# A hybrid decoder layer on one core: small vectors requested by GpSimd, x scaled on ScalarE, and K tiles grouped 3, 4, 4, 5

## The chip, the cores and the metric

One core of a Trainium2 chip runs the whole program. The engines are TensorE (PE in the profile; its weight loads are PEld), VectorE (DVE), ScalarE (ACT), GpSimd (POOL) and SyncE (SP), which here issues the loads from memory. The metric is the time of one launch in microseconds (us), the median of several executions. Differences under about 0.2% (2.6 us) are not distinguishable from none.

## What is computed

One layer on 256 tokens of width 2048. The part that matters here is its head:

```
mod = silu(c) @ w_mod + b_mod                  # w_mod 2048 x 12288; six rows of 2048
sh1, sc1, g1, sh2, sc2, g2 = split(mod)
h = rmsnorm(x, norm_mix) * (1 + sc1) + sh1
proj = h @ w_in                                # w_in 2048 x 5660
# proj feeds four token mixers: gated linear attention, gated DeltaNet, pooling, forgetting attention
y = concat(mixers) @ w_out;  x = x + g1 * y
h = rmsnorm(x, norm_ffn) * (1 + sc2) + sh2
x = x + g2 * (silu(conv(h @ w_gate)) * (h @ w_up)) @ w_down
out = rmsnorm(x, norm_final)
```

All arithmetic is float32 in effect: each weight tile is split into a rounded high part and the low remainder, and a product is made of three matmuls (high-high, high-low, low-high).

## The kernel before

The 2048 inputs of the first projection are 16 tiles of 128, the K tiles. They are visited in four groups (`GROUPS`, four tiles each). For a group the first stage needs the shift and scale (sh1, sc1) of its tiles, which is a product of one row, silu(c), with all 2048 rows of w_mod: `mods4` loads 16 tiles `wm` (128 partitions, two runs of 512 columns, 512 KB each), and VectorE adds each into `ga` with the factor from silu(c) (line 103). When the 16th is in, 8 products of `ga` with a column of ones (16 matmul instructions, "ext<-ones,ga") turn the sums into columns `md`, three VectorE rows finish `md`, ScalarE makes h of each tile from the transposed x, and `split` writes its high and low part into `bigA`. Only then can matmuls of this group's tiles run.

What a group's tiles feed is of two kinds. `gdn(g)` multiplies them with 1536 columns of w_in into six accumulators `acc` that stay in PSUM over all groups. `extras(g)` visits the last `TAKE[g]` of 16 column pairs (256 columns each) and adds the group's part to their sums in SBUF (rows "pr<-ext,pr" on VectorE). What is not visited early is made up after the last group, between the steps of the mixers. Each piece of w_in is loaded as `wr` (five buffers), and `split` gives `wh` (ScalarE cast, line 115) and `wl` (VectorE subtraction, line 100), three buffers each, before the matmul (line 97). While a group's matmuls run, the generator `nxt` brings in the next group's `wm` tiles, one per step.

Small vectors (convolution weights, norms, biases, constants `ct`, the rows `hrow`, and the 28 narrow columns of w_in as `wsm`) are requested by `rest` and `small_load` during the first group, on SP's queue among the large loads; `rest` also transposes some of them on TensorE. `small` and `gates` use them at the last group. GpSimd has 23 rows of its own in the whole program.

The order on each engine is set by a list scheduler from the order of the code and its own estimate of times, and each engine then runs its list in that order: an instruction that waits holds up everything behind it on its engine.

Of the kernel before, what the change touches and what calls it, by code (L numbers as in the profile page):

```python
# [42 lines left out]
K_N = K_LV + 128  # L43


GROUPS = ((0, 4), (4, 4), (8, 4), (12, 4))
NG = len(GROUPS)

TAKE = (16, 12, 11)

ORDER = "gpfd"

ON_PE, PE_RATE = "s0 s1 h0", 0.38
ON_DVE, DVE_RATE = "h1 g0 g1", 0.69


def _consts():
# [16 lines left out]
def trunk_kernel(ctx: ExitStack, tc: tile.TileContext, x, c, w_mod, b_mod, norm_mix, norm_ffn, w_in,  # L74
# [153 lines left out]
    with ExitStack() as ph:  # L228
# [59 lines left out]
        with ExitStack() as st:  # L288
# [29 lines left out]
                act(flat(pr[:, 0:8]), xt[:, t], AF.Square, accum_out=ssm[:, t:t + 1])  # L318
            tsc(ssm[:, 2:4], ssm[:, 0:2], 1.0 / D, EPS, ALU.mult, ALU.add)
            G.tensor_tensor(out=ssm[:, 0:2], in0=ssm[:, 2:4], in1=mhalf[:, 0:2], op=ALU.pow)  # L320
# [12 lines left out]


            def mods(g):
                for k0 in range(GROUPS[g][0], sum(GROUPS[g]), 4):
                    yield from mods4(k0, min(4, sum(GROUPS[g]) - k0))

            def mods4(k0, nk):
                n = nk * P  # L340

                def f(ga):
                    b = ext()
                    for i in range(2 * nk):
                        mm(b[:, i:i + 1], ga[:, i * P:i * P + P], ones[:, 0:1])
                    md = sp.tile([P, 2 * nk], F32, name="md", tag="md", bufs=2, padded_shape=[P, 16])
                    tt(md[:, 0:nk], b[:, 0:nk], bm(0, k0, nk), ALU.add)
                    tt(md[:, nk:], b[:, nk:2 * nk], bm(1, k0, nk), ALU.add)
                    tt(md[:, nk:], md[:, nk:], nmix[:, k0:k0 + nk], ALU.mult)
                    for kk in range(nk):  # L350
                        k = k0 + kk
                        h = sp.tile([P, T], F32, name="h", tag="h", bufs=2)
                        act(h, xnT[:, k], AF.Identity, scale=md[:, nk + kk:nk + kk + 1], bias=md[:, kk:kk + 1])
                        split(HL[:, k, 0:T], HL[:, k, T:], h)
                views = [wm_v[:, k, 0:2 * D].rearrange("p (s n) -> p s n", n=D)[:, :, P * k0:P * k0 + n]
                         for k in range(KT)]
                ga = keep.tile([P, 2 * n], F32, name="ga", tag="ga", padded_shape=[P, 1024])
                for k in range(KT):
                    wm = sp.tile([P, 2 * n], F32, name="wm", tag="wm", bufs=5, padded_shape=[P, 1024])
                    last_wm[0] = nc.sync.dma_start(wm.rearrange("p (s n) -> p s n", n=n), views[k])  # L360
                    accumulate(ga, wm, k)
                    if k == KT - 1:
                        with tc.high_priority():
                            f(ga)
                    yield

            def rest():
                nc.sync.dma_start(wlr[0:16], gla_w_lr[0])
                nc.sync.dma_start(wlr[28:29], gla_b_lr)
                nc.sync.dma_start(r2[0:48], gdn_conv[0].rearrange("j (k p) -> (j k) p", p=P))  # L370
                nc.sync.dma_start(r2[48:52], pool_scale[0].rearrange("(k p) -> k p", p=P))
                nc.sync.dma_start(r2[52:53], gla_norm)
                nc.sync.dma_start(r2[53:54], gdn_norm)
                nc.sync.dma_start(ct, cst[:, P:K_N])
                row = lambda ap: ap.partition_broadcast(P).rearrange("p o h -> p (o h)")
                nc.sync.dma_start(hrow[:, 0:4], row(gdn_a_log))
                nc.sync.dma_start(hrow[:, 4:8], row(gdn_dt_bias))
                nc.sync.dma_start(hrow[:, 8:12], row(fox_f_bias))
                nc.sync.dma_start(r3, ffn_conv_w[0, 0:2].rearrange("j (k p) -> (j k) p", p=P))
                nc.sync.dma_start(r4[0:NF], ffn_conv_w[0, 2].rearrange("(k p) -> k p", p=P))  # L380
                nc.sync.dma_start(r4[NF:], ffn_conv_b[0].rearrange("(k p) -> k p", p=P))
                b = ext()
                PE.transpose(b[:, 0:54], r2, ident[0:54, 0:54])
                S_.copy(V2, b[:, 0:54])
                b = ext()
                PE.transpose(b[:, 0:2 * NF], r3, ident[:2 * NF, :2 * NF])
                PE.transpose(b[:, 2 * NF:4 * NF], r4, ident[:2 * NF, :2 * NF])
                S_.copy(V3, b[:, 0:3 * NF])
                S_.copy(CB, b[:, 3 * NF:4 * NF])
                S_.copy(idr, ident)  # L390
                S_.copy(ngr, K(K_NEG))
                for i, m_ in enumerate(up + lw):
                    G.tensor_scalar(out=m_, in0=K(K_LV), scalar1=float(i + 1), scalar2=None, op0=ALU.is_equal)


            def small_load():
                nc.sync.dma_start(wsm[:, :, 0:16], wi_v[:, :, C_LR:C_LR + 16])
                nc.sync.dma_start(wsm[:, :, 16:24], wi_v[:, :, C_B:C_B + 8])
                nc.sync.dma_start(wsm[:, :, 24:28], wi_v[:, :, C_FF:C_FF + 4])
                split(wsh, wsl, wsm)  # L400

            def small():
                o = ext()[0:28, 0:T]
                for k in range(KT):
                    mm(o, wsh[:, k], HL[:, k, 0:T], start=k == 0, stop=False)
                    mm(o, wsh[:, k], HL[:, k, T:], start=False, stop=False)
                    mm(o, wsl[:, k], HL[:, k, 0:T], start=False, stop=k == KT - 1)
                S_.copy(smT[0:28], o)

            def gdn(g):  # L410
                k0, nk = GROUPS[g]
                for k2 in range(k0, k0 + nk, 2):
                    for c3 in range(3):
                        wh, wl = load_split(wi_v, k2, 2, C_QKV + 512 * c3, 512)
                        for kk in range(2):
# [22 lines left out]
            def pair(p, g0, g1):  # L438
                c0, tok, dst, scale = pairs[p]
                k0, k1 = GROUPS[g0][0], sum(GROUPS[g1 - 1])  # L440
                a = ext().rearrange("p (f t) -> p f t", t=T)
                for ka in range(k0, k1, 4):
                    kb = min(ka + 4, k1)
                    wh, wl = load_split(wi_v, ka, kb - ka, c0, 256)
# [12 lines left out]
                    yield  # L457
# [46 lines left out]

            bgt = lambda: bgp.tile([P, 512], F32, name="bgt", tag="bgt")
            bg = [marked(jobs(ON_PE, bgt)), jobs(ON_DVE, None)]
            for _ in mods(0):
                pass
            hold = [last_wm[0]]
            for g in range(NG):  # L510
                nxt = mods(g + 1) if g < NG - 1 else iter(())
                with tc.issue_after(hold[0].ins):
# [1 line left out]
                        small()  # L514
                        gates()
                    for i, _ in enumerate(gdn(g)):
                        next(nxt, None)
                        if g == 0 and i == 2:
                            rest()
                            small_load()  # L520
                    if g == NG - 1:
                        break
                    for _ in extras(g):
                        next(nxt, None)
# [605 lines left out]
```

## Time and profile before

| | us |
|---|---|
| median of 3 runs (1309.63 to 1311.2) | 1309.63 |
| profiled execution, its own time | 1305.91 |
| span of the profiled execution | 1304.1 |
| TensorE busy | 1251.1 (96%) |
| VectorE busy | 893.8 (69%) |
| ScalarE busy | 638.1 (49%) |
| GpSimd busy | 23.5 (2%) |

The page gives busy time by engine, the span in 40 slices, the chain of work that ended last, and groups of equal instructions with mean duration and the idle time ahead of them. Besides it the trace answers by window (busy time, granted TensorE clock, and memory traffic in a stretch) and by timeline (instructions in order of time, with what ended the idle time ahead of each). 1.8 us of the profiled execution lie outside its span.

### The profile page before, as it was taken

The numbers are of one execution on the slowest core, as the hardware profiler recorded it, in microseconds if no ns is written. First come the engines' busy times: TensorE is split into PE (matmuls) and PEld (weight loads), VectorE is DVE, ScalarE is ACT, GpSimd is POOL, SyncE is SP. The second block draws the span as 40 slices with busy tenths as digits, with TensorE's granted clock in tenths as the row PEclk, the third lists the DMA queues.
The fourth block names the chain that finished last, engine by engine and source line by source line (L and its number), as shares of the span: only waits on it lengthen the run. The fifth ranks groups of instructions, "written<-read, shape, count | busy, mean of one in ns | idle before, by whom it ended". The sixth has DMA issues, their size and how long they took to land.

```text
span 1304.1 us, 20373 instructions
## 1 busy us (share of the span) xinstructions
PE 1251.1 (96%) x7927; PEld 1094.0 (84%) x7927; DVE 893.8 (69%) x1201; ACT 638.1 (49%) x1000; POOL 23.5 (2%) x31
## 2 busy tenths in 40 slices
PE   2799999999999999999999999999999999999996
PEld 1799999898876788888888888888888888888896
DVE  7679797989763397676656565765666597974543
ACT  3455344774354444565545554555555454443432
POOL 0200000010000100000000000000000000000000
PEclk8799999999999999999999999999999999999998
DMA  8999998796567997466666666666666699875652
GB/s 324 287 367 376 321 335 295 257 335 216 163 236 242 325 331 262 146 183 189 186 187 191 182 176 197 191 184 188 190 184 181 193 372 366 316 249 193 193 180 81
DMA packets 174231, 311.94 MB, mean 239 GB/s; under 512 B 16172, under 2 KB 65331, under 8 KB 173495
## 3 DMA queue, kind: packets, MB, share of 16 engines
q1 hardware_dynamic: 174135, 310.65, 73.3%
q8 instruction: 62, 1.02, 0.3%
q14 instruction: 34, 0.28, 0.1%
HBM read 308.51 MB, written 2.10 MB: 238 GB/s over the span
## 4 chain that ended last, share of the span: by engine, by line
PE 92%; DMA 5%; DVE 1%; ACT 1%; issue 1%; SPq 1%; POOLq 0%; ACTq 0%; DVEq 0%
PE fpt L97 57%; PE ext L97 16%; PE wot L97 5%; PE acc L97 4%; PE gdt L97 4%; DMA wm<-in_w_mod_dram 4%; PE bgt L97 3%; PE oxt L97 2%; DVE ga L103 1%; DMA wr<-in_w_in_dram 1%; DMA wsm<-in_w_in_dram 0%; ACT xT L1011 0%; DVE wl L100 0%; ACT wh L115 0%; PE oxt L873 0%
## 5 line engine op out<-in xcount | busy, mean ns | idle before, releaser
L100 DVE TENSOR_TENSOR wl<-wr,wh 128x1024 fp32r<-128x1024 f32 x384 | 468.4, 1223 | 294.2 <-ACT wh L115 293.2
L115 ACT CAST wh<-wr 128x1024 fp32r<-128x1024 f32 x384 | 402.5, 1051 | 491.4 <-PE fpt L97 306.6
L97 PE MATMUL fpt<-bigA,wh 128*128 128x512 f32 x1408 | 485.7, 397 | 2.1 <-DVE bigA L103 2.1
L97 PE MATMUL fpt<-bigA,wl 128*128 128x256 f32 x1408 | 376.2, 281 | 0.0
L97 PEld LDWEIGHTS fpt<-bigA,wh 128*128 128x128 f32 x1408 | 261.1, 188 | 62.5 <-issue 2.2
L97 PEld LDWEIGHTS fpt<-bigA,wl 128*128 128x128 f32 x1408 | 259.7, 188 | 4.8
L103 DVE SCALAR_TENSOR_TENSOR ga<-wm,cond,ga 128x1024 f32<-128x1024 f32 x139 | 177.8, 1279 | 11.3 <-DMA wm<-in_w_mod_dram 10.3
L97 PE MATMUL fpt<-wl,AH 128*128 128x512 f32 (+1 forms) x440 | 152.9, 348 | 0.0
L97 PE MATMUL fpt<-wh,AL 128*128 128x512 f32 (+1 forms) x440 | 152.5, 347 | 0.0
L97 PE MATMUL fpt<-wh,AH 128*128 128x512 f32 (+1 forms) x440 | 142.6, 348 | 0.0
L97 PE MATMUL ext<-bigA,wh 128*128 128x256 f32 x768 | 137.1, 280 | 0.0
L97 PEld LDWEIGHTS ext<-bigA,wh 128*128 128x128 f32 x768 | 117.3, 189 | 3.1 <-DVE dS L100 0.8
L97 PE MATMUL ext<-bigA,wl 128*128 128x256 f32 x384 | 107.4, 280 | 1.7 <-DVE wl L100 1.7
L97 PEld LDWEIGHTS fpt<-wh,AH 128*128 128x128 f32 x440 | 83.3, 189 | 10.8 <-ACT wh L115 0.2
L97 PEld LDWEIGHTS fpt<-wh,AL 128*128 128x128 f32 x440 | 83.3, 189 | 10.6 <-issue 0.2
L97 PEld LDWEIGHTS fpt<-wl,AH 128*128 128x128 f32 x440 | 83.3, 189 | 10.5 <-issue 0.2
L97 PEld LDWEIGHTS ext<-bigA,wl 128*128 128x128 f32 x384 | 72.1, 188 | 3.0 <-DVE wl L100 1.9
L97 PE MATMUL acc<-bigA,wh 128*128 128x256 f32 x384 | 69.0, 286 | 3.5 <-ACT bigA L115 2.8
L97 PE MATMUL ext<-wh,bigA 128*128 128x256 f32 (+1 forms) x320 | 69.5, 309 | 0.0
L97 PE MATMUL wot<-wh,bigA 128*128 128x512 f32 (+1 forms) x256 | 63.0, 337 | 0.0
L97 PEld LDWEIGHTS acc<-bigA,wh 128*128 128x128 f32 x384 | 59.6, 195 | 3.9 <-ACT bigA L115 2.9
L97 PEld LDWEIGHTS ext<-wh,bigA 128*128 128x128 f32 x320 | 53.0, 193 | 5.5 <-ACT wh L115 1.7
(340 smaller groups left out, 1187.4 us busy)
## 6 DMA issues: line engine op xcount, KB each, us to landing
wm<-in_w_mod_dram SPq DMA_DIRECT2D x192, 512.0 KB, 6.3
wr<-in_w_in_dram SPq DMA_DIRECT2D x88, 512.0 KB, 9.1
wr<-in_ffn_w_gate_dram SPq DMA_DIRECT2D x88, 512.0 KB, 4.0
wr<-in_ffn_w_up_dram SPq DMA_DIRECT2D x88, 512.0 KB, 3.9
wr<-in_ffn_w_down_dram SPq DMA_DIRECT2D x88, 512.0 KB, 4.4
wr<-in_w_out_dram SPq DMA_DIRECT2D x32, 512.0 KB, 4.4
xt<-in_x_dram SPq DMA_DIRECT2D x2, 1024.0 KB, 7.1
bigC<-in_x_dram SPq DMA_DIRECT2D x2, 1024.0 KB, 10.5
```

The lines of the kernel that those rows point to most:

```text
L97: PE.matmul(o, lhsT=l, rhs=r, start=start, stop=stop, skip_group_check=True)
L100: V.tensor_tensor(out=o, in0=a, in1=b, op=op)
L103: V.scalar_tensor_tensor(out=o, in0=a, scalar=s, in1=b, op0=op0, op1=op1)
L115: S_.copy(hi, src)
```

## The change

- The groups are 3, 4, 4 and 5 K tiles. A group of five is cut by `runs` into runs of at most four for the shift and scale and for the column pairs (3 and 2) and of at most two for the DeltaNet columns (2, 2 and 1). `ahead` advances the next group's generator once per run of that group.
- 16, 13 and 12 column pairs are visited early in place of 16, 12 and 11.
- The two VectorE multiplications that scale x by its norm become four ScalarE activations on half rows.
- All 16 small requests leave SP's queue for GpSimd's. They stand behind a GpSimd instruction that is new, the last multiplication of the second group's `md`. The split of `wsm` moves into `small`, and the transposes and masks of `rest` behind the third group.

```
-GROUPS = ((0, 4), (4, 4), (8, 4), (12, 4))
+GROUPS = ((0, 3), (3, 4), (7, 4), (11, 5))
-TAKE = (16, 12, 11)
+TAKE = (16, 13, 12)
+def runs(k0, n, most):
+    m = -(-n // most)
+    cut = [k0 + (n * i + m - 1) // m for i in range(m + 1)]
+    return [(a, b - a) for a, b in zip(cut, cut[1:])]
...
-            for t in range(NT):
-                tsc(xt[:, t], xt[:, t], ssm[:, t:t + 1], None, ALU.mult)
+            for hs in (slice(0, D // 2), slice(D // 2, D)):
+                for t in range(NT):
+                    act(xt[:, t, hs], xt[:, t, hs], AF.Copy, scale=ssm[:, t:t + 1])
...
-                    tt(md[:, nk:], md[:, nk:], nmix[:, k0:k0 + nk], ALU.mult)
+                    if k0 == GROUPS[1][0]:
+                        asked[0] = G.tensor_tensor(out=md[:, nk:], in0=md[:, nk:], in1=nmix[:, k0:k0 + nk], op=ALU.mult)
+                    else:
+                        tt(md[:, nk:], md[:, nk:], nmix[:, k0:k0 + nk], ALU.mult)
...
+            def rest_load():
+                G.dma_start(wlr[0:16], gla_w_lr[0])
...
+            def ahead(g, nxt):
+                for _ in range(len(runs(*GROUPS[g + 1], 4)) if g < NG - 1 else 0):
+                    next(nxt, None)
...
                     for i, _ in enumerate(gdn(g)):
-                        next(nxt, None)
-                        if g == 0 and i == 2:
-                            rest()
-                            small_load()
+                        ahead(g, nxt)
...
+                if g == 0:
+                    with tc.issue_after(asked[0].ins):
+                        small_load()
+                        rest_load()
+                if g == 2:
+                    rest()
```

On SP, in the first group, the last small requests stood ahead of the fourth piece of w_in (`wr`); before:

```order
L379 DMA r3_112<-in_ffn_conv_w_dram 88x128
L380 DMA r4_113<-in_ffn_conv_w_dram 44x128
L381 DMA r4_113<-in_ffn_conv_b_dram 44x128
L397 DMA wsm_115<-in_w_in_dram 128x16x16
L398 DMA wsm_115<-in_w_in_dram 128x16x8
L399 DMA wsm_115<-in_w_in_dram 128x16x4
L155 DMA wr_417<-in_w_in_dram 128x2x512
L360 DMA wm_447<-in_w_mod_dram 128x2x512
```

and now, from the third piece on:

```order
L162 DMA wr_340<-in_w_in_dram 128x2x512
L374 DMA wm_337<-in_w_mod_dram 128x2x512
L162 DMA wr_373<-in_w_in_dram 128x512
L374 DMA wm_370<-in_w_mod_dram 128x2x512
L162 DMA wr_394<-in_w_in_dram 128x512
L374 DMA wm_391<-in_w_mod_dram 128x2x512
```

The 16 small requests are gone from this queue, and the odd third tile of the group is loaded in single-tile pieces.

On ScalarE, the rows that use the small vectors moved from the first group into the second. `wsh` is the cast of `wsm`, `ngr` that of a piece of `ct`, `ea` the exponential of `hrow`; now they stand so among the casts of the weight pieces:

```order
L122 CAST wh_929<-wr_927 128x1024
L444 COPY pr_92<-ext_859 128x512
L122 CAST wsh_116<-wsm_115 128x448
L444 COPY pr_92<-ext_885 128x512
L122 CAST wh_963<-wr_961 128x1024
L122 CAST wh_996<-wr_994 128x1024
L122 CAST wh_1029<-wr_1027 128x1024
L122 CAST wh_1062<-wr_1060 128x1024
L407 CAST ngr_91<-ct_85 128x128
L119 ACT_TABLE_LOAD
L119 ACTIVATE ea_2385<-hrow_89 128x4
L122 CAST wh_1095<-wr_1093 128x1024
```

Here `wh_929` and the next five are the six pieces of DeltaNet weights of the second group; `wsh` stands behind the first of them, `ngr` and `ea` behind the fifth.

On VectorE, the rows that finish the first group's `md` were and are:

```order
L100 TENSOR_TENSOR wl_280<-wr_277,wh_279 128x1024
L100 TENSOR_TENSOR wl_314<-wr_311,wh_313 128x1024
L100 TENSOR_TENSOR md_257<-ext_248,V1_73 128x4 x2
L107 TENSOR_SCALAR ga_307<-wm_308,cond_77 128x1024
L100 TENSOR_TENSOR md_257<-md_257,V1_73 128x4
```

```order
L107 TENSOR_TENSOR wl_276<-wr_273,wh_275 128x1024
L107 TENSOR_TENSOR md_257<-ext_250,V1_73 128x3 x2
L107 TENSOR_TENSOR wl_310<-wr_307,wh_309 128x1024
L107 TENSOR_TENSOR md_257<-md_257,V1_73 128x3
L114 TENSOR_SCALAR ga_303<-wm_304,cond_77 128x1024
```

The second subtraction now stands between the rows of `md`, and the first row of the next group's sum behind them.

More of the change, by code (lines that the diff above doesn't have):

```diff
@@ L335, in mods @@
             def mods(g):
-                for k0 in range(GROUPS[g][0], sum(GROUPS[g]), 4):
-                    yield from mods4(k0, min(4, sum(GROUPS[g]) - k0))
+                for k0, nk in runs(*GROUPS[g], 4):
+                    yield from mods4(k0, nk)
+            asked = [None]
             def mods4(k0, nk):
@@ L396, in small_load, with small @@
             def small_load():
-                nc.sync.dma_start(wsm[:, :, 0:16], wi_v[:, :, C_LR:C_LR + 16])
-                nc.sync.dma_start(wsm[:, :, 16:24], wi_v[:, :, C_B:C_B + 8])
-                nc.sync.dma_start(wsm[:, :, 24:28], wi_v[:, :, C_FF:C_FF + 4])
+                for o, c, n in ((0, C_LR, 16), (16, C_B, 8), (24, C_FF, 4)):
+                    G.dma_start(wsm[:, :, o:o + n], wi_v[:, :, c:c + n])
+            def small():
                 split(wsh, wsl, wsm)
-            def small():
                 o = ext()[0:28, 0:T]
@@ L410, in gdn @@
             def gdn(g):
-                k0, nk = GROUPS[g]
-                for k2 in range(k0, k0 + nk, 2):
+                for k2, nk in runs(*GROUPS[g], 2):
                     for c3 in range(3):
-                        wh, wl = load_split(wi_v, k2, 2, C_QKV + 512 * c3, 512)
-                        for kk in range(2):
+                        wh, wl = load_split(wi_v, k2, nk, C_QKV + 512 * c3, 512)
+                        for kk in range(nk):
                             k = k2 + kk
@@ L441, in pair @@
                 a = ext().rearrange("p (f t) -> p f t", t=T)
-                for ka in range(k0, k1, 4):
-                    kb = min(ka + 4, k1)
-                    wh, wl = load_split(wi_v, ka, kb - ka, c0, 256)
+                for ka, nk in sum((runs(*GROUPS[g], 4) for g in range(g0, g1)), []):
+                    kb = ka + nk
+                    wh, wl = load_split(wi_v, ka, nk, c0, 256)
                     for f in range(2):
@@ L523, in trunk_kernel @@
                     for _ in extras(g):
-                        next(nxt, None)
+                        ahead(g, nxt)
                 for _ in nxt:
```

27 lines of the change are left out of this document (13 added, 14 removed).

## The prediction

> **What bounds the kernel now.** I read the page first, then the windows, then the timeline of the first 220 us.
>
> ```profile
> PE 1251.1 (96%) x7927; PEld 1094.0 (84%) x7927; DVE 893.8 (69%) x1201; ACT 638.1 (49%) x1000; POOL 23.5 (2%) x31
> ```
>
> TensorE is busy for all but 53 us of 1304.1, and both instruction orders hold the same 7427 matmuls, so only its idle time, its slow clock and new waits can move the end. The windows (columns: busy time of PE, PEld, DVE, ACT, POOL, then granted clock, share and rate of memory traffic) say where the loss is.
>
> ```profile
> 10.00:20.00 10.00, 4.62 (x18) 3.35 (x19) 8.20 (x10) 3.22 (x6) 0.70 (x1) 1.00 0.98 348
> 20.00:30.00 10.00, 2.61 (x16) 1.91 (x15) 9.35 (x9) 2.77 (x5) 0.00 (x0) 0.72 0.96 338
> 30.00:42.00 12.00, 3.54 (x16) 3.49 (x16) 9.71 (x12) 4.46 (x7) 0.00 (x0) 0.50 1.04 372
> 42.00:48.10 6.10, 6.08 (x26) 5.75 (x27) 3.88 (x6) 3.75 (x9) 4.10 (x6) 0.50 0.61 93
> 50.00:60.00 10.00, 8.50 (x72) 8.13 (x71) 5.44 (x5) 3.76 (x6) 1.57 (x3) 1.00 0.97 335
> 60.00:75.00 15.00, 13.31 (x110) 12.91 (x109) 11.85 (x11) 6.84 (x9) 0.00 (x0) 1.00 1.08 366
> 42.00:98.20 56.20, 52.65 (x405) 51.42 (x406) 38.42 (x37) 26.39 (x38) 7.32 (x12) 0.91 0.99 321
> 98.20:162.70 64.50, 62.81 (x550) 62.62 (x550) 53.85 (x57) 29.55 (x37) 0.00 (x0) 1.00 1.02 348
> 162.70:215.20 52.50, 52.50 (x449) 52.50 (x449) 48.88 (x55) 22.27 (x26) 0.00 (x0) 1.00 0.98 330
> 215.20:262.00 46.80, 45.52 (x379) 40.86 (x378) 41.95 (x88) 29.57 (x55) 1.45 (x3) 1.00 0.79 254
> ```
>
> Until 42 us memory runs at 338 to 372 GB/s while TensorE is mostly idle: the head waits for loads. From 42 to 48 the clock is 0.50 and traffic falls to 93 GB/s. TensorE idles another 1.50 and 1.69 us up to 75. Afterwards it is full or nearly so, with VectorE at 48.88 of 52.50 and memory at 330 to 348 GB/s close behind. The timeline shows the steps of the head and the ends of the first three groups' sums (the `md` rows).
>
> ```profile
> 4.20 24.69 SPq L360 DMA_DIRECT2D wm<-in_w_mod_dram  x16
> 17.39 1.23 ACT L328 COPY bigC<-ext 128x512 f32<-128x512 f32 x2 [5.92 <-PE ext L327]
> 22.30 1.09 ACT L328 COPY bigC<-ext 128x512 f32<-128x512 f32 x2 [0.24 <-PE ext L327]
> 31.47 0.88 SPq L368 DMA_DIRECT2D wlr<-in_gla_w_lr_dram  x1
> 34.28 1.29 DVE L103 SCALAR_TENSOR_TENSOR ga<-wm,cond,ga 128x1024 f32<-128x1024 f32 x1 [0.47 <-DMA wm<-in_w_mod_dram]
> 35.71 3.54 PE L97 MATMUL ext<-ones,ga 128*128 128x1 f32 x16 [12.94 <-DVE ga L103]
> 39.29 0.23 DVE L100 TENSOR_TENSOR md<-ext,V 128x4 f32<-128x4 f32 x2
> 40.10 0.16 DVE L100 TENSOR_TENSOR md<-md,V 128x4 f32<-128x4 f32 x1
> 42.02 1.65 PE L97 MATMUL acc<-bigA,wh 128*128 128x256 f32 x6 [2.77 <-ACT bigA L115]
> 43.66 0.40 SPq L397 DMA_DIRECT2D wsm<-in_w_in_dram  x1
> 47.79 2.07 SPq L155 DMA_DIRECT2D wr<-in_w_in_dram  x1
> 50.87 0.57 ACT L115 CAST wsh<-wsm 128x448 fp32r<-128x448 f32 x1 [3.86 <-DMA wsm<-in_w_in_dram]
> 98.12 0.23 DVE L100 TENSOR_TENSOR md<-ext,V 128x4 f32<-128x4 f32 x2 [1.08 <-PE ext L97]
> 162.70 0.22 DVE L100 TENSOR_TENSOR md<-ext,V 128x4 f32<-128x4 f32 x2
> 215.15 0.22 DVE L100 TENSOR_TENSOR md<-ext,V 128x4 f32<-128x4 f32 x2
> ```
>
> The sixteenth wm tile ends VectorE's wait at 34.28; sums, columns and h follow, and the first matmul of a product starts at 42.02. The sums are made against this execution (span 1304.1, itself 1305.91 with 1.8 outside the span) and then taken off the median, 1309.63, which lies 3.7 above it.
>
> **Three tiles first.** Sixteen tiles of 384 in place of 512 KB are 2.10 MB less. At 355 GB/s, between the rows' 338 and 372, that is 5.9 us. The last sum row is shorter:
>
> ```profile
> L103 DVE SCALAR_TENSOR_TENSOR xt<-bigC,V,xt 128x253 f32<-128x253 f32 x12 | 5.6, 469 | 0.0
> L112 ACT ACTIVATE pr<-xt 128x2048 f32<-128x2048 f32 x2 | 3.8, 1910 | 2.8 <-DMA xt<-in_x_dram 2.8
> 168.70 1.28 DVE L103 SCALAR_TENSOR_TENSOR ga<-wm,cond,ga 128x1024 f32<-128x1024 f32 x1
> 169.90 0.68 DVE L100 TENSOR_TENSOR pr<-ext,pr 128x512 f32<-128x512 f32 x1
> 170.50 1.21 DVE L100 TENSOR_TENSOR wl<-wr,wh 128x1024 fp32r<-128x1024 f32 x1
> 171.63 0.42 DVE L100 TENSOR_TENSOR bigA<-h,bigA 128x256 fp32r<-128x256 f32 x1
> 171.96 1.28 DVE L103 SCALAR_TENSOR_TENSOR ga<-wm,cond,ga 128x1024 f32<-128x1024 f32 x1
> ```
>
> From 469 ns at 253 columns and 1280 at 1024 it costs 1.05 ns a column, so 768 columns save 0.27. Twelve column products in place of 16, at 3.54/16 = 0.22, save 0.9. Against it, the subtraction that now stands between the md rows pushes their last one back: 0.15 + 1.13 where 0.81 stands now, +0.5. The first product matmul comes 6.6 earlier, at 35.4.
>
> **ScalarE scales x.** Four half rows at 1.91/2 are 3.8 us. They lie in ScalarE's 5.92 of idle time before 17.39; the last copy of the transposed x, begun by 23, may end 2 us later, and its reader (h) starts only after md, past 33. VectorE's rows that leave the head were followed by waits for loads. Cost and gain nothing; without the 8 us of cover, up to 2.
>
> **The first group.** From 42.02 to 98.12 are 56.1 us for 384 matmuls. The pitch, from 162.70 to 215.15 with 432 matmuls, is (52.45 - 1.8)/432 = 0.117, where 1.8 is for 16 column products at full clock (half of 0.22 each). So 46.7 is work; 9.4 is excess: 3.05 for 6.1 us at half clock, 3.2 idle in the 50:60 and 60:75 rows, the rest small transposes and dips. The changed order has 288 matmuls here: 33.7 + 1.8. The clock will again have dropped (TensorE idles before the sums), so 3.0 stays. Of the other 6.4 I take half off: SP no longer spends 31.47 to 47.79 mostly on small requests, and the fourth wr no longer waits for them until 47.79. That gives 41.7, and the group's sums end at 77.1; between 38.5 and 44.9.
>
> On the clock the Trainium skill (TensorE: Matmul & The Clock Gate, The HAM clock gate) says some 3.4 us of sustained work release it; the row has 6.1. By the rule 1.3 us less would be lost; the row decides.
>
> **The second group.** 492 matmuls: 57.6 + 1.8, and 1.0 of excess as in 98.12 to 162.70 (528: 63.6 of 64.6). It ends at 137.5. VectorE, by the steps of the next part, has 15 sums, 19 long and 5 short subtractions and 10 adds: 18.0 + 21.5 + 4.3 + 6.0 and 2.8 of small rows, 52.6; it was 53.85 and stays under TensorE. The last md row on GpSimd is 0.5 us longer than on VectorE by its nearest row (below), while TensorE still has pairs of the old group to do: nothing.
>
> **Five tiles in two pieces.** This is where the early gain is partly given back. TensorE has 460 matmuls and 20 column products: 53.8 + 2.2 = 56.0. VectorE's steps, from start to start in the rows above, are 1.20 for a sum, 0.60 for an add, 1.13 for a subtraction, 0.33 for bigA; by 1.05 ns a column a sum of 768 steps 0.93, of 512 0.66. The order holds 15 + 15 of these sums, their two first rows (1.0), 19 subtractions, 13 adds, 7 bigA and 0.8 of md: 14.0 + 9.9 + 1.0 + 21.5 + 7.8 + 2.3 + 0.8 = 57.3. VectorE becomes the longer one. It can't be gapless (48.88 of 52.50 is the most it had), so I take 59.0, between 57.3 and 61.6 (57.3 at that share). The third sums' end: 196.5.
>
> At that point 1240 matmuls are done, against 1344 at 215.15; 104 at 0.117 are 12.2, so the same work stood at 203.0 before. Small transposes still to come take off 0.4. **Sum: 203.0 - 0.4 - 196.5 = 6.1 us earlier.** After it TensorE was busy for 45.52 of 46.80, and what is left of pairs fills the mixers as before, so the gain stays. The span would be 1298.0, the median 1303.5.
>
> **GpSimd's requests.** This price the trace doesn't show. ScalarE takes wsh, ngr and ea in order, so a late request stops every wh behind it. From the end of the second group's sums TensorE has 132 matmuls until it needs wh_963, 15.4 us; less about 2 for md and the first request and 1.6 for two casts, the three wsm may take 11.7 us. For ea, behind thirteen requests, the same count (228 matmuls) leaves 21.8. From below: SP's three took 7.2 (43.66 to 50.87). From above:
>
> ```profile
> L393 POOL TENSOR_SCALAR mk<-ct 128x128 uint8<-128x128 f32 x12 | 7.3, 615 | 31.8 <-DMA ct<-in_cst_dram 31.2
> L320 POOL TENSOR_TENSOR ssm<-ssm,mhalf 128x2 f32<-128x2 f32 x1 | 0.7, 696 | 11.5 <-DVE ssm L109 11.5
> ```
>
> GpSimd takes 615/128 = 4.8 ns a column; if it made each of the 2048 short runs of a wsm request at that pace, three would take 29.5. I take the lower end, since the transfers are the same ones: hidden.
>
> **Rivals.** (1) *GpSimd's requests are late.* For it: 6144 runs of 64, 32 and 16 bytes from an engine that has made no request so far, and ScalarE's order, which lets nothing pass wsh. Against it: SP's 7.2. It decides from 11.7 us for three wsm; beyond that TensorE idles one for one, and from 17.8 the whole gain is gone. At 29.5 it costs 17.8: 1321.3. Where it ends on the slow side, taken halfway from 17.8 to 29.5 at 23.7, 12.0 are lost: 1315.5. The first thing seen would be ACT's wsh or ea idle behind a DMA.
> Of this the Trainium skill (DMA: Bandwidth & Descriptors, Anatomy of one DMA) gives about 2.0 us of fixed cost for a request made by GpSimd. If they followed one another without overlap, thirteen would be an estimated 26 us, 4 over the 21.8, and the time 1307.7; no run here shows it yet.
>
> (2) *Memory becomes the bound.* The second group and the two pieces need 8.4 + 10.7 + 0.8 and 10.5 + 10.0 MB, 40.4 in all, for which the sum allows 119.4 us, 338 GB/s. The rows have 348 and 330, and runs get shorter (1536 and 1024 bytes in place of 2048). At 330 it takes 122.4, 3.0 lost; at 322 the gain is gone. I put it at 326: 4.5 lost, 1308.0.
>
> (3) *More than the sum.* VectorE hides its excess in TensorE's (3.0 back) and all 3.2 of the small idles go: 1297.3. For it: the 162.70:215.20 row, where VectorE at 93% cost TensorE nothing.
>
> **How the numbers follow.** Chances: forecast 0.53, 1303.5, its own range 1299 to 1308; late requests 0.22, 1306 to 1321; memory 0.13, 1306 to 1313; more 0.12, 1296 to 1299. Within 0.2%, what a measurement can't tell from none, is 1307.0 to 1312.2. Faster: 0.47 of the forecast, 0.04 of memory, 0.02 of the late requests, all of "more": 0.65. Slower: 0.13 of the late requests, 0.02 of memory, 0.01 of the forecast: 0.16. Same: the rest, 0.19. The range leaves out about 0.06 at the low end (half of "more") and 0.08 at the high end (the later of the late requests): 1297 to 1316.
>
> **What would show it.** The first acc matmul at 35 to 36; md of the second group at 75 to 80, of the third at 135 to 140; the last piece's md at 194 to 200 with VectorE near 95% in between; wsh without a wait. The sum is wrong if wsh or ea waits over 12 us, if TensorE's idle time grows between 75 and 200 by more than 6 us, or if the head's rate falls with the shorter runs.

## The result and the profile after

The changed kernel took 1331.75 us (median; 1329.17 to 1336.33), the kernel before 1309.63 on the same chip. The ratio is 1.0178, with a 95% interval of 1.0156 to 1.0200: 22 us slower, where 6 faster was forecast and 1316 was the upper end of the range. The profiled execution has a span of 1330.6, against 1304.1 before; these lie 26.5 apart, since the one before was 3.7 below its median. What follows accounts for the 26.5.

The timeline of the changed kernel answers to the steps of the head and the `md` rows (columns: start, duration, engine, line, operation; in brackets the idle time before it):

```profile
31.77 0.23 DVE L107 TENSOR_TENSOR md<-ext,V 128x3 f32<-128x3 f32 x2
35.68 1.65 PE L104 MATMUL acc<-bigA,wh 128*128 128x256 f32 x6 [3.95 <-ACT bigA L122]
76.17 0.23 DVE L107 TENSOR_TENSOR md<-ext,V 128x4 f32<-128x4 f32 x2 [1.40 <-PE ext L104]
77.10 3.73 POOL L414 DMA_DIRECT2D wsm<-in_w_in_dram  x3
89.34 0.57 ACT L122 CAST wsh<-wsm 128x448 fp32r<-128x448 f32 x1
91.02 0.51 POOL L395 DMA_DIRECT2D r<-in_ffn_conv_b_dram  x1
141.45 0.22 DVE L107 TENSOR_TENSOR md<-ext,V 128x4 f32<-128x4 f32 x2
204.60 0.23 DVE L107 TENSOR_TENSOR md<-ext,V 128x2 f32<-128x2 f32 x2 [0.35 <-PE ext L104]
```

The head is where it was forecast. GpSimd's sixteen requests run from 77.10 to 91.5, and nothing waits for them. The last two `md` rows are late, by 4 and by 8 us. The larger loss comes after them. Two windows split the first 473 and 498 us at the last matmul of `acc`, and end with the first matmul of the second chunk of w_out (`wot`). Columns: window, its length, busy time and matmuls of PE, then PEld, DVE, ACT and POOL, granted clock, share and rate of memory traffic. First the kernel before, then the change:

```profile
0.00:239.61 239.61, 203.40 (x1662) 199.18 (x1663) 191.80 (x230) 109.09 (x151) 9.67 (x20) 0.94 0.97 326
239.61:472.94 233.33, 231.90 (x1700) 186.45 (x1699) 163.07 (x287) 122.92 (x269) 10.49 (x7) 1.00 0.75 256
```

```profile
0.00:237.13 237.13, 202.02 (x1615) 195.80 (x1616) 190.86 (x253) 110.05 (x155) 24.65 (x37) 0.95 0.97 322
237.13:498.11 260.98, 247.45 (x1747) 199.06 (x1746) 175.40 (x307) 129.95 (x288) 8.87 (x7) 0.96 0.73 246
```

The second window is 27.65 us longer. TensorE idles 13.5 in place of 1.4 us there (12.1 more) and is busy for 15.5 us more. Of these, 47 more matmuls take 5.5 (at 0.117): column pairs that were done ahead of it before. The other 10 are longer times of the same matmuls. The clock explains 8.1 of them: it was 0.50 during 16.2 us of work (rows below), and at 1.00 throughout in the kernel before. The last 2 are not accounted for. From the first `wot` matmul to the end both kernels take nearly the same: 831.2 and 832.5 us. So the loss is a loss of TensorE's time beside the mixers. The chain of waits shows where half of the idle time lies; the change (start, duration, what; steps under 0.3 us left out):

```profile
458.59 1.06 PE bgt L104 x8
460.03 0.39 SPq L192
460.52 0.44 SPq L192
461.01 10.90 DMA wr<-in_w_out_dram
471.93 1.05 ACT wh L122
473.02 1.22 PE ext L104 x2
474.28 24.00 PE ext L104 x94
498.29 1.83 PE wot L104 x8
```

The kernel before, same place (the longer pieces):

```profile
441.66 1.88 PE bgt L97 x16
443.54 2.51 PE gdt L97 x24
446.31 0.86 PE bgt L97 x2
447.17 1.15 PE oxt L97 x7
448.77 3.25 PE ext L97 x14
452.02 0.86 PE bgt L97 x2
452.88 3.91 PE ext L97 x17
457.44 4.37 PE ext L97 x19
462.46 10.55 PE ext L97 x46
```

`bgt` are the background products of w_mod, and `ext` here those of the first chunk of w_out. The loads of w_out stand behind the last w_mod tile on SP, and a w_mod tile is asked for only when a `bgt` matmul has freed its buffer. In the kernel before, the background ends while the mixers are still at work, so w_out's first loads and half of its first products lie between the mixers' own matmuls (`gdt`, `oxt`). In the change the background ends together with the mixers. Most of the load (10.9 us) then stands bare, and so do the 24 us of products. The windows of 20 us here, first the change:

```profile
460.00:480.00 20.00, 13.25 (x54) 9.23 (x52) 9.95 (x15) 9.77 (x19) 1.96 (x2) 0.74 0.94 355
```

and the kernel before:

```profile
460.00:480.00 20.00, 20.00 (x90) 16.44 (x90) 19.52 (x23) 10.37 (x16) 0.00 (x0) 1.00 0.87 319
```

The change's clock was 0.50 in three places of the mixers' stretch. The last is shown in two rows, idle and at work:

```profile
284.49:291.31 6.82, 6.82 (x33) 6.82 (x33) 4.18 (x16) 0.00 (x0) 0.95 (x1) 0.50 0.90 327
434.67:438.08 3.41, 3.41 (x14) 2.79 (x13) 0.69 (x1) 0.00 (x0) 0.00 (x0) 0.50 1.00 402
468.81:473.02 4.21, 0.00 (x0) 0.00 (x0) 0.02 (x1) 1.04 (x1) 0.00 (x0) 0.50 1.01 369
473.02:479.05 6.03, 5.99 (x13) 4.31 (x14) 5.75 (x5) 2.19 (x3) 0.00 (x0) 0.50 0.82 292
```

So the wait for w_out, 6.36 us in one piece, is followed by 6 us of work at half clock, which cost 3 more. The Trainium skill (TensorE: Matmul & The Clock Gate, The HAM clock gate) says that an idle stretch of some 3.4 us puts the array back to half clock. The last place agrees with it. At the other two no such stretch came first: the longest waits in the 10 us ahead of them are 1.04 and 1.68 us.

### The profile page after: what moved, and what is told of

Same layout as the page of the kernel before. It is cut to its first block, busy times and chain, and to the rows that moved or that the text cites. A ratio compares the mean times of both kernels' runs of the same rounds, so it can differ in the third digit from the quotient of the medians.

```text
span 1330.6 us, 20558 instructions
## 1 busy us (share of the span) xinstructions
PE 1266.7 (95%) x7927; PEld 1104.5 (83%) x7927; DVE 898.7 (68%) x1238; ACT 646.1 (49%) x1023; POOL 36.8 (3%) x48
## 4 chain that ended last, share of the span: by engine, by line
PE 86%; DMA 8%; DVE 3%; ACT 2%; issue 1%; SPq 0%; POOL 0%; ACTq 0%; DVEq 0%; POOLq 0%
PE fpt L104 56%; PE ext L104 12%; PE wot L104 5%; DMA wr<-in_w_in_dram 4%; PE acc L104 3%; PE gdt L104 3%; DMA wm<-in_w_mod_dram 3%; PE bgt L104 2%; PE oxt L104 2%; DVE ga L110 2%; DMA wr<-in_w_out_dram 1%; DVE wl L107 1%; ACT wh L122 1%; DMA xt<-in_x_dram 1%; ACT xT L1033 0%
## 5 line engine op out<-in xcount | busy, mean ns | idle before, releaser
L107 DVE TENSOR_TENSOR wl<-wr,wh 128x1024 fp32r<-128x1024 f32 (+2 forms) x403 | 471.3, 1172 | 310.7 <-ACT wh L122 309.5
L122 ACT CAST wh<-wr 128x1024 fp32r<-128x1024 f32 (+2 forms) x403 | 406.0, 1010 | 513.5 <-PE fpt L104 310.3
L110 DVE SCALAR_TENSOR_TENSOR ga<-wm,cond,ga 128x1024 f32<-128x1024 f32 (+2 forms) x154 | 181.0, 1176 | 14.6 <-DMA wm<-in_w_mod_dram 13.8
L104 PE MATMUL ext<-bigA,wh 128*128 128x256 f32 x768 | 141.5, 285 | 0.4 <-DVE gv L107 0.4
L104 PE MATMUL ext<-bigA,wl 128*128 128x256 f32 x384 | 110.2, 287 | 0.5 <-DVE wl L107 0.2
L104 PE MATMUL ext<-wh,bigA 128*128 128x256 f32 (+1 forms) x320 | 74.1, 319 | 8.5 <-ACT wh L122 6.8
```

The lines of the kernel that those rows point to most:

```text
L104: PE.matmul(o, lhsT=l, rhs=r, start=start, stop=stop, skip_group_check=True)
L107: V.tensor_tensor(out=o, in0=a, in1=b, op=op)
L110: V.scalar_tensor_tensor(out=o, in0=a, scalar=s, in1=b, op0=op0, op1=op1)
L122: S_.copy(hi, src)
```

## The experiments

Each changed kernel ran in turn with the kernel before on one chip. The chips differ from experiment to experiment (medians of the kernel before 1308.40 to 1309.63), so kernels are compared by their ratios. The table holds: column-pair tiles left for the mixers and in how many pieces they are visited (counted from the groups and from TAKE); from the traces the start of the last addition of a pair's product, of the last `bgt` matmul, of the last `Y` (the DeltaNet mixer's last output) and of the first `wot` matmul, in us; and the median with its ratio to the kernel before.

| kernel | tiles / pieces | last pair | last bgt | last Y | first wot | median, ratio |
|---|---|---|---|---|---|---|
| before | 100 / 25 | 382.4 | 437.9 | 454.8 | 472.9 | 1309.63 |
| the change | 108 / 39 | 417.1 | 459.8 | 462.7 | 498.1 | 1331.75, 1.0178 |
| requests_and_scale_only | 100 / 25 | 381.3 | 437.4 | 454.0 | 472.9 | 1309.01, 0.9994 |
| groups_only | 108 / 39 | 421.5 | 460.9 | 474.2 | 492.5 | 1328.40, 1.0142 |
| pace_25_39 | 108 / 39 | 410.8 | 464.4 | 452.1 | 499.0 | 1333.05, 1.0181 |
| pace_24_of_39 | 108 / 39 | 435.0 | 437.8 | 481.9 | 509.5 | 1341.45, 1.0250 |
| w_out_asked_by_gpsimd | 108 / 39 | 415.9 | 458.2 | 465.5 | 493.5 | 1326.25, 1.0134 |
| before_pace_24_of_25 | 100 / 25 | 435.2 | 438.0 | 490.0 | 508.3 | 1334.69, 1.0202 |
| take_only | 92 / 23 | 389.1 | 446.0 | 469.4 | 482.5 | 1314.48, 1.0034 |
| left_over_in_twos | 100 / 41 | 389.3 | 439.8 | 458.0 | 479.8 | 1315.86, 1.0056 |
| take_11_10 | 108 / 27 | 391.6 | 452.3 | 454.2 | 490.3 | 1324.03, 1.0113 |
| take_11_10_in_twos | 108 / 43 | 394.8 | 459.5 | 450.4 | 492.5 | 1328.08, 1.0144 |

**Which part of the change.** One kernel has the groups and TAKE alone, the other all but these.

```
groups_only: the change with small_load and rest as in the kernel before (nc.sync),
             x scaled by tsc on VectorE, md by tt on VectorE
requests_and_scale_only:
-GROUPS = ((0, 3), (3, 4), (7, 4), (11, 5))
+GROUPS = ((0, 4), (4, 4), (8, 4), (12, 4))
-TAKE = (16, 13, 12)
+TAKE = (16, 12, 11)
```

> The kernel before with the groups 3, 4, 4, 5, their runs and the 16, 13 and 12 column pairs; the small vectors stay on SP and x is scaled on VectorE. Theory P (pace): the background loads of w_mod are advanced by 0.38 and 0.69 tile steps for each step of the last column pairs, of which there are now 39 in place of 25, because a group of five is visited in two runs; they crowd out the pairs' loads, and the pairs, w_out and the start of the product with w_out come late. By it this kernel is slow as well, 1325 to 1335 us, with the wot tiles' first DMA issue near 498 us. Theory Q (the moved requests): GpSimd's requests or the scaling reorder the rest; then this kernel is near the kernel before, 1300 to 1312 us.

> The changed kernel with groups 4, 4, 4, 4 and 16, 12 and 11 column pairs again: only GpSimd's requests and the scaling on ScalarE are left of the change. Theory P (pace): 25 steps in the last column pairs as before, so 1304 to 1311 us, a little faster or the same. Theory Q (the moved requests): 1322 to 1335 us.

Measured: 1328.40, ratio 1.0142 (1.0125 to 1.0158), and 1309.01, ratio 0.9994 (0.9982 to 1.0007). The groups and TAKE make most of the loss, 19 of the 22 us; theory Q is out. The second kernel holds a surprise. One row each from the views of the tiles `md`, `bgt` and `wot` (count, duration in ns, first and last start in us), first the kernel before, then it:

```profile
L100 DVE TENSOR_TENSOR md<-ext,V x8: 150/154/163, 39.3 to 215.2; 128x4 f32<-128x4 f32 x8
L97 PE MATMUL bgt<-wm,cond x192: 592/592/617, 245.5 to 437.9; 128*32 128x512 f32 x192
L97 PE MATMUL wot<-wh,bigA x256: 279/335/797, 472.9 to 541.0; 128*128 128x512 f32 x64, 128*128 128x256 f32 x64
```

```profile
L107 DVE TENSOR_TENSOR md<-ext,V x8: 151/153/163, 36.3 to 206.5; 128x4 f32<-128x4 f32 x8
L104 PE MATMUL bgt<-wm,cond x192: 592/592/617, 237.7 to 437.4; 128*32 128x512 f32 x192
L104 PE MATMUL wot<-wh,bigA x256: 279/336/797, 472.9 to 541.1; 128*128 128x512 f32 x64, 128*128 128x256 f32 x64
```

With the same groups and the same work it reaches the last `md` 8.7 us earlier (206.5 against 215.2) and starts the background 7.8 us earlier, and `wot` starts at 472.9 in both. A lead at the mixers' start was worth nothing here.

**The background's pace.** Theory P blamed the background loads, handed out per piece. Two kernels change the rates of the change, one the rate of the kernel before, and one takes w_out's first loads off SP.

```
pace_25_39:             PE_RATE 0.38 -> 0.244, DVE_RATE 0.69 -> 0.442
pace_24_of_39:          PE_RATE 0.38 -> 0.62
before_pace_24_of_25:   PE_RATE 0.38 -> 0.96, in the kernel before
w_out_asked_by_gpsimd (`load` and `load_split` pass the issuing engine on):
...
-wh, wl = load_split(wo_v, ks[0], nk, c0, w)
+wh, wl = load_split(wo_v, ks[0], nk, c0, w, G if n == 0 else nc.sync)
```

> The changed kernel with the two background rates multiplied by 25/39 (0.244 and 0.442 in place of 0.38 and 0.69), so that the background loads advance by as much over all last column pairs as in the kernel before. Theory P (pace): the 25 us return, and the gain of some 0 to 2 us that is left when the last group's sums end shows or not: 1303 to 1313 us. Theory Q (the moved requests) and theory R (more pairs left over for the mixers, 108 tiles of pairs in place of 100): no change, 1328 to 1336 us.

> The changed kernel with TensorE's background rate 0.62 in place of 0.38 (VectorE's as it is), so that 24 of its 24 steps of w_mod are handed out with the 39 visits of the last column pairs and none is left for after them. Theory G (gate): what sets the start of the wot products is the last bgt matmul, since w_out's first loads stand behind the last w_mod tile on SP and follow it by 1.2 us, and the wot products follow by 32 to 40 us. In the change the visits end at 417 us and 10 steps of 4.3 us follow; here the visits end later, by up to 10 x 1.9 = 19 us, but nothing follows: last bgt at 430 to 440, wot at 468 to 478, 1300 to 1312 us. Theory M (the mixers' own chain or the lost head start sets the end): 1326 to 1336 us.

> The kernel before with TensorE's background rate 0.96 in place of 0.38, so that all 24 steps are handed out with its 25 visits. Theory G: the last bgt matmul moves from 437.9 to 405 to 420, and the mixers' tail, done at 455, sets the end: 1297 to 1308 us. Theory M: 1306 to 1314 us.

> The changed kernel with the eight loads of w_out's first 512 columns requested by GpSimd, not behind the w_mod tiles on SP. TensorE's order stays, with the first product of w_out behind the last bgt matmul. Theory G: only the 14 us between the last bgt matmul (459.8) and the first such product (474.3) shrink, by 8 to 13 us: 1319 to 1324 us. Theory M: no change, 1328 to 1336 us.

Measured: 1333.05 (1.0181; 1.0160 to 1.0201), 1341.45 (1.0250; 1.0229 to 1.0270), 1334.69 (1.0202; 1.0171 to 1.0233) and 1326.25 (1.0134; 1.0119 to 1.0150). Theory P falls. A slower background lets the pairs end 6 us earlier (410.8) and ends itself 5 later (464.4). A faster one ends at 437.8, as wanted, but then the mixers end at 481.9 and nothing is left to fill their waits: TensorE idles 15.0 of the 71.7 us from the last `bgt` to `wot`. The kernel before suffers the same: with its whole background handed out early it is 25 us slower. Both want TensorE's time, and the rate only decides which is late. Taking w_out's loads off SP won 5.5 us, a little less than theory G asked for: the row "461.01 10.90 DMA" is part of the loss, not all of it.

**How the groups are laid.** Theory R blamed the volume left over, theory C the cut visits of the five tiles, theory T the phases ahead.

```
take_14_13:      the change, TAKE = (16, 14, 13)     100 tiles, 37 pieces
take_12_11:      the change, TAKE = (16, 12, 11)     116 tiles, 41 pieces
groups_3_4_5_4:  groups 3, 4, 5, 4, TAKE = (16, 13, 11)
groups_3_5_4_4:  groups 3, 5, 4, 4, TAKE = (16, 13, 12)
groups_4_4_3_5:  groups 4, 4, 3, 5, TAKE = (16, 12, 11)
```

> The changed kernel with 16, 14 and 13 column pairs visited early in place of 16, 13 and 12, so that 100 tiles of pairs are left after the last group as in the kernel before, and not 108. The last pairs are then 37 steps, not 39. Theory R (the left-over pairs): the 48 matmuls of 0.117 us, 5.6 us, leave the mixers' stretch but 4 to 5 of them return ahead of it, and if the late pairs are what holds the tail, 1310 to 1322 us. Theory P (pace): the pace is still 1.48 times that of before, 1326 to 1336 us.

> The changed kernel with 16, 12 and 11 column pairs early, as before, in place of 16, 13 and 12: 116 tiles of pairs are left for the mixers in 41 pieces, and the two phases ahead lose 4 and 4 to 5 tiles of pairs of work. Theory C (cuts): as slow or slower, 1328 to 1340 us. Theory T (VectorE's load ahead of the mixers is what costs): 1318 to 1328 us, since a pair more in each phase cost 8 to 9 us.

> The changed kernel with groups 3, 4, 5, 4 and 16, 13 and 11 column pairs early. The group of five is now the third; the last has four tiles, visited in one piece, and the left-over visits are 29 pieces (25 before, 39 in the change) with 101 tiles of pairs. Theory C (cuts): most of the 22 us returns, 1302 to 1314 us. Theory T (the phases ahead): a group of five still makes VectorE the longer one ahead of the mixers; 1320 to 1335 us.

> The changed kernel with groups 3, 5, 4, 4 and 16, 13 and 12 column pairs early: the left-over visits are 26 pieces with 95 tiles of pairs. Five tiles' sums fall beside the first group's 288 matmuls and will hold them up by some 8 us. Theory C (cuts): 1302 to 1316 us. Theory T: 1320 to 1335 us.

> The changed kernel with groups 4, 4, 3, 5 and 16, 12 and 11 early pairs: the last group of five without the three at the head, 111 tiles of pairs left over in 42 pieces at most. If the five at the end are the cause, 1322 to 1340 us; if the three at the head are, 1305 to 1315 us.

Measured: 1341.14 (1.0243), 1336.06 (1.0207), 1341.31 (1.0254), 1323.89 (1.0118) and 1336.24 (1.0196). Neither theory holds for all five: the first and the third lie outside every range given, the second went as C has it, the fourth as T. Pairs moved ahead (take_14_13) cost more there than they freed: `acc` ends at 243.7, 6.6 us later. Fewer of them ahead (take_12_11) end `acc` at 233.3, and `wot` starts at 503.2 all the same, 5 later than in the change. The group of three at the head isn't needed for the loss (4, 4, 3, 5 has it), and no place of the five tiles that was tried avoids it. Since groups, volume and pieces change together here, none of the five separates a cause; the next ones were made on the kernel before.

**Volume and cuts alone.** Groups of four throughout, small vectors on SP. TAKE sets how many tiles are left over. The cut visits the last group's four tiles of each pair as two and two.

```
take_only:           TAKE = (16, 13, 12)     92 tiles
take_11_10:          TAKE = (16, 11, 10)    108 tiles, as in the change
left_over_in_twos:
-for ka in range(k0, k1, 4):
-    kb = min(ka + 4, k1)
+cuts = [ka for ka in range(k0, k1, 4)]
+if g1 == NG:
+    cuts.append(14)
+for ka, kb in zip(cuts, cuts[1:] + [k1]):
take_11_10_in_twos:  both of the last
```

> The kernel before with 16, 13 and 12 column pairs visited early in place of 16, 12 and 11; groups of four. Left over are 92 tiles of pairs, not 100. If the early pairs themselves are the cause (VectorE too full ahead of the mixers), 1315 to 1330 us; if not, 1304 to 1312 us.

> The kernel before (groups of four, small vectors on SP) with one edit: the last group's four tiles of each column pair, visited beside the mixers, are loaded, split and multiplied as two pieces of two tiles instead of one piece of four; the background pace is advanced once for both. Same matmuls, 16 more loads, 16 more casts and subtractions. Theory C (cuts): the mixers' stretch is paced by how many columns of weights its three wh and wl buffers hold at a time, so small pieces slow the pairs; 1316 to 1330 us, with ext matmuls of the pairs left undone at 380 us. Theory T (timing of the phases ahead, not the cut): 1306 to 1313 us.

> The kernel before with 16, 11 and 10 column pairs early in place of 16, 12 and 11: groups of four, whole visits, and 108 tiles of pairs left over as in the change (100 before); 48 matmuls, 5.6 us, move from ahead of the end of the acc products to behind it. If the volume alone is the cause, 1320 to 1332 us; if only volume and cuts together are, 1307 to 1314 us.

> The kernel before with 16, 11 and 10 early pairs and the last group's visits in two pieces of two tiles: volume and cuts of the change with groups of four, small vectors on SP. If the two together make the loss, 1322 to 1335 us; the sum of the two taken apart would be 1316 plus what the volume alone costs. If the group boundaries themselves matter, less.

Measured: 1314.48 (1.0034; 1.0018 to 1.0050), 1315.86 (1.0056; 1.0039 to 1.0074), 1324.03 (1.0113; 1.0086 to 1.0140) and 1328.08 (1.0144; 1.0126 to 1.0163). Moving 48 matmuls, 5.6 us of TensorE's work, from ahead of the mixers to beside them costs 15.6 us. Cut visits cost 6 alone and 4 on top. Together they make 19.7 of the change's 22 us, without a group of three or five and without a moved request. But volume has no fixed price: take_only moves 48 matmuls the other way and is 5.3 us slower too. The trace of take_11_10 repeats that of the change. Its windows, the last two those of a half clock that comes while TensorE is busy throughout:

```profile
237.00:490.30 253.30, 242.29 (x1746) 194.91 (x1746) 173.92 (x300) 126.87 (x272) 9.70 (x7) 0.97 0.73 250
460.00:480.00 20.00, 13.93 (x51) 10.87 (x52) 13.04 (x11) 6.78 (x7) 0.00 (x0) 0.74 0.97 347
268.00:272.34 4.34, 4.34 (x40) 4.34 (x40) 2.82 (x3) 4.29 (x6) 0.00 (x0) 1.00 1.07 378
272.34:275.75 3.41, 3.41 (x17) 3.41 (x18) 2.53 (x4) 2.03 (x5) 0.00 (x0) 0.50 1.04 366
```

and two of the waits in its chain:

```profile
453.34 11.57 DMA wr<-in_w_out_dram
464.93 1.05 ACT wh L115
```

Its mixers end when they did before, and the background 14.4 us later:

```profile
L97 PE MATMUL bgt<-wm,cond x192: 592/593/617, 243.0 to 452.3; 128*32 128x512 f32 x192
L112 ACT ACTIVATE Y<-gdt,oss x8: 349/370/385, 448.5 to 454.2; 128x128 f32<-128x128 f32 x8
```

What changed is the order of TensorE's matmuls. The windows from the last `bgt` to the first `wot`, with the rows of `gdt` (mixer matmuls) alone, for the kernel before, take_11_10 and the change (columns of PE, PEld, DVE and ACT):

```profile
437.95:472.94 34.99, 7.07 (x56) 5.86 (x56) 2.18 (x3) 4.79 (x24) 1.00 0.91 327
452.35:490.30 37.95, 0.64 (x4) 0.51 (x4) 1.13 (x2) 1.15 (x4) 0.87 0.99 374
459.85:498.11 38.26, 1.26 (x8) 0.89 (x8) 1.50 (x2) 1.14 (x4) 0.87 0.98 364
```

In the kernel before, 56 of the mixers' matmuls stand behind the last background product, and w_out's first load comes in while most of them run. In take_11_10 four do, in the change eight; the others went ahead. This moves the last `bgt`: from the end of `acc` to it, take_11_10 has 48 matmuls of pairs, 52 `gdt` and 10 `oxt` more than the kernel before. With requests and scaling alone 56 stand behind it, as before.

The distance from the last `bgt` to the last `Y` is the cover that w_out's loads and first products have: 16.9 us in the kernel before, 16.6 with requests and scaling alone, 1.9 here, 2.9 in the change, below nothing with volume and cuts. With the groups alone it is 13.3, and there the mixers themselves end 19 us late. It doesn't decide alone: take_only and left_over_in_twos have 23.4 and 18.2 and are slower all the same, and with much more (pace_24_of_39) the mixers are late. In the kernels of the table `wot` follows the last `bgt` by 32 to 40 us, except where the mixers end far behind the background (pace_24_of_39, before_pace_24_of_25).

**Leaving the sixteenth tile out.** Both kernels leave the last of the sixteen K tiles out of the column pairs' products (a part of the work is missing: 96 matmuls, 11.2 us); the change then has whole visits of four tiles in its last group. The change then visits 23 pieces; the expectation below says 27.

```
the change:  k0, k1 = GROUPS[g0][0], min(sum(GROUPS[g1 - 1]), KT - 1)
             runs(GROUPS[g][0], min(GROUPS[g][1], 4), 4)
before:      k0, k1 = GROUPS[g0][0], min(sum(GROUPS[g1 - 1]), KT - 1)
```

> The changed kernel, leaving the last of the sixteen K tiles out of the products of the column pairs (not out of those of the acc tiles): the last group's visits are then one piece of four tiles, 27 pieces in all in place of 39, and 96 matmuls fewer, 11.2 us at 0.117. If the loss is just TensorE's work, 1318 to 1323 us. If the cut visits are the cause, they come on top: 1306 to 1315 us. If late pairs have a threshold behind which the tail fills badly, under 1305 us.

> The kernel before, leaving the last K tile out of the products of the column pairs: 96 matmuls and a quarter of the last visits' casts and subtractions fewer, as many pieces as before. If the stretch is bound by TensorE's work, 1296 to 1301 us; if by the mixers' chain or the background jobs, 1303 to 1311 us.

Measured: 1317.25 (1.0062; 1.0042 to 1.0082) and 1313.40 (1.0027; 1.0014 to 1.0040). The change gains 14.5 us, a little more than its work, and ends between the first two ranges; the two designs stand 3.9 apart instead of 22, and the kernel before gets slower by 4 with 11 us of work less, outside both of its ranges. Its background ends at 424.8, its mixers at 469.2, 14 later than with all the work, and up to `wot` TensorE idles 9.1 us in place of 1.4. The stretch is a balance: less work in it doesn't shorten it either.

**An attempt at a faster kernel.** Requests and scaling alone have a lead of 8.7 us that they lose; a higher background rate was to keep it.

```
requests_scale_pace_46:  requests_and_scale_only, PE_RATE 0.38 -> 0.46
```

> Groups of four with GpSimd's requests and x scaled on ScalarE, and TensorE's background rate 0.46 in place of 0.38: 11 of 24 steps with the visits instead of 9. If the background's pace after the visits is what eats the lead of 7.1 us, up to 6 us of it return, 1302 to 1307 us; if pairs, background and mixers are balanced as they stand, 1308 to 1316 us.

Measured: 1324.52 (1.0115; 1.0089 to 1.0142), outside both ranges. Two steps of 24 handed out earlier made the background end at 459.1, later than without (437.4), with the pairs' end at 398.9 for 381.3. No kernel here beats the one before.

## Why the prediction was wrong

- **Three tiles first** was right in place and size: the first matmul of a product at 35.68, forecast 35.4. Its cause was half mistaken. With the groups alone this matmul stands at 38.5, with the requests and the scaling alone at 38.3, and at 42.02 before. So what was costed at nothing in the head, the scaling and SP's freed queue, brought as much as the smaller group; the two were not taken apart.
- **The first group** was right: its sums end at 76.17, forecast 77.1.
- **The second group** was sized wrong: 65.3 us, forecast 60.4. The matmuls of the group were counted rightly, but TensorE idles 4.5 us in this stretch, in six waits for rows of ScalarE and VectorE of 0.4 to 1.7 us; the sum had 1.0 of excess, taken from the kernel before. (The 7427 matmuls of the whole program are 7927 on both pages; nothing hangs on it.)

The windows of the change from the first product matmul to the first of these `md` rows, and from `md` to `md`:

```profile
35.68:76.17 40.49, 39.58 (x305) 38.28 (x306) 31.68 (x33) 18.57 (x28) 0.00 (x0) 0.92 1.07 373
76.17:141.45 65.28, 60.77 (x514) 59.26 (x514) 54.58 (x57) 31.63 (x42) 22.28 (x29) 1.00 1.05 332
141.45:204.60 63.15, 58.42 (x478) 58.05 (x477) 58.60 (x78) 26.03 (x33) 0.00 (x0) 0.95 0.97 316
```

- **Five tiles in two pieces**: VectorE is the longer engine, as forecast, and its busy time of 58.60 lies within the 57.3 to 61.6 given. The 63.15 us lie above that range: VectorE at 93% was costed, TensorE's 4.7 us of idle time (3.6 of it one wait for VectorE's sums) and the clock of 0.95 (3.2 us) were not. Together with the group before, the third sums' end came at 204.60 in place of 196.5. The 6.1 us were gone there, and 2.0 more. One of the signs named for a wrong sum showed: between 75 and 200 TensorE's idle time grew by more than 6 us, to 9.2 in these two groups from 1.7 in the two that match them before.
- **"After it TensorE was busy for 45.52 of 46.80, and what is left of pairs fills the mixers as before, so the gain stays"** is the step that failed most: some 20 of the 22 us. Two assumptions stood in it. That a lead stays falls with requests_and_scale_only, which has one of 8.7 us and starts `wot` at the same 472.9. That left-over pairs fill the mixers at no cost falls with take_11_10, where 5.6 us of pairs cost 15, and the mixers' matmuls that covered w_out's first load went ahead of the background. The 8 tiles more were in the count of matmuls (104 against 1344) but had no price of their own, and the 14 further pieces had none at all. The row that spoke against it was there: with TensorE at 231.9 of 233.3 us beside the mixers, there was no room to fill.
- **GpSimd's requests are hidden**, as forecast: three `wsm` requests took 3.73 us to ask for, and ScalarE's `wsh` at 89.34 and the vectors behind it waited for nothing. Rival (1) fell, but by a little: the last `wsm` landed by 88.4, 11 us after 77.10, where SP's 7.2 had been taken and 11.7 allowed. Of the Trainium skill's 2.0 us for each such request (DMA: Bandwidth & Descriptors, Anatomy of one DMA) the trace shows no sum: the thirteen small ones were asked for between 80.82 and 91.5, 10.7 us in all, waits included, so their fixed costs overlap.
- **Memory becomes the bound**, rival (2), has rows for it: the second group and the two pieces ran at 332 and 316 GB/s, 324 together, where the sum needed 338 and the rival had 326. The first group ran at 373. TensorE's waits there ended with rows of ScalarE and VectorE, but ScalarE's casts in turn waited up to 3.2 us for pieces of w_in. No experiment separates memory from VectorE.
- The slower side held 0.16, nearly all of it in late requests and memory. A rival for the mixers' stretch was missing, though the change hands it 8 tiles more.

What stays open: why 5.6 us of pairs put the mixers' last matmuls ahead of the last background product. The order of TensorE's matmuls is made anew for each kernel, no run changes it alone, and requests_scale_pace_46 shows that a small shift can move this end by 20 us. A rival is left. All seven kernels that have groups of four and another pace, volume or cut than the kernel before are slower than it, by 4 to 25 us, whichever way they differ. So its settings may lie at a best point, and the loss may be the price of leaving it, not of the pairs as such. How much of the 15 us is such an order, and how much any order would pay, isn't settled.

## What to carry to other kernels

Where an engine is busy for 232 of 233 us beside a latency-bound chain, work handed to that stretch is not hidden: price it, and price the work queued behind it. Look for the last job that gates the next stage's loads, count what of the chain is left behind it to cover them (here 56 matmuls, 17 us), and see whether the change leaves it there. A lead at the start of such a stretch counts only if the stretch's own end moves with it, so compare the end, not the start.

## What was not expected of the hardware

- A wait of 6.36 us cost TensorE half as much again: the clock was 0.50 for the 6 us of work that followed. Long waits were not needed for it: in the same stretch the half clock came behind waits of at most 1.04 and 1.68 us, and in take_11_10 behind none.
- Sixteen requests on GpSimd, three of them with 2048 short runs each, took 14.4 us in all, 3.9 of it waits: 0.5 to 0.6 us for a small one, 1.15 to 1.41 for one with short runs. The latter landed 8.1 to 8.4 us after they were asked for.
- The masks on GpSimd (`mk`, twelve of 128 columns), made of the vectors that it had asked for, took 0.94 us each; in the kernel before they took 0.62. The durations fall in two kinds (shortest, median, longest in ns; first the change, then before):

```profile
L409 POOL TENSOR_SCALAR mk<-ct x12: 519/1166/1383, 93.7 to 104.3; 128x128 uint8<-128x128 f32 x12
L393 POOL TENSOR_SCALAR mk<-ct x12: 523/527/1587, 43.8 to 51.2; 128x128 uint8<-128x128 f32 x12
```

In the change seven of the twelve took 1.17 to 1.38 us, and beside each of them VectorE ran rows of 1024 columns with two large inputs (`wl` or `ga`) for 0.8 to 1.5 us; beside the five short ones it ran for at most 0.4. In the kernel before the one long mask had a `ga` row beside it for 1.2 us. No experiment separates the two engines.
